# Loads of k, q and running sums for later query blocks issued from ScalarE's queue, in a hybrid decoder layer on one Trainium2 core

## The chip, the cores and the metric

The kernel runs on one core of one Trainium2 chip. A core has TensorE (PE in the profile; its weight loads have a row of their own, PEld), VectorE (DVE), ScalarE (ACT), GpSimd (POOL) and SyncE (SP), each with its own instruction queue that is worked off in order, and 16 DMA engines that move data between DRAM and the on-chip buffers. A DMA is started by an instruction in the queue of one of the engines. The metric is device time in microseconds of one launch. Before the change it is 2859.11 us, the median of 3 runs (2857.32 to 2863.01).

## The reference

One layer of a decoder trunk for 2048 positions of width 1024, in float32. A mixer with three head groups reads one projection; a SwiGLU block and a gated per-layer embedding follow. What matters here is the third head group, attention with a forget bias, six heads of 64, swept in query blocks, and what runs beside it:

```python
h = h + mixer(rmsnorm(h))                  # SSD group | RG-LRU group | attention, then w_out
u = rmsnorm(h, norm2_g)
h = h + (silu(u @ w_gate) * (u @ w_up)) @ w_down        # d_ff = 2816
u = rmsnorm(h, norm3_g)
h = h + sigmoid(u @ w_ple_gate + b) * (p @ w_ple_proj)
...
cum = cumsum(log_f)                                     # attention, per head
logits = q @ k.T / 8 + cum[q, None] - cum[None, k]      # k up to the end of the query block
probs = softmax(where(causal, logits, -inf))
out = probs @ v
```

## The kernel before

Positions lie on the free axis, in four blocks of 512 (`tb` 0 to 3, `TB` = 512); features lie on the 128 partitions. Every dense product is done as three matmuls (`mm3`, L199 to L201): weight and activation are each split in a high and a low half, and high·high, high·low and low·high are summed in PSUM. A weight tile goes through `wst` (DMA, L183, two buffers), ACT writes its high half (L189), POOL its low half (L190), and three such `w` tiles exist at a time. One weight is 24 matmuls of 512 columns.

Phase 1 makes k, q, v and the recurrent group, phase 1b the SSD group and the attention of query block 0. Phase 3 (`phase3`, L828) is the rest, and the change lies in it: for `tb` 0, 1, 2 the feed-forward of block `tb` is the main stream, and the attention of query block `tb+1` is a side stream (`attention_t`, L691). `attention_t` is a generator; `mm3` calls it forward by a few steps after each group of three matmuls. So the stretches of the trace with attention beside the feed-forward are three: 750 to 1160 us (query block 1), 1360 to 1680 us (block 2) and 1900 to 2290 us (block 3). They are called the first, second and third stretch below. The last feed-forward has no attention beside it.

For one head, `attention_t` does this. `load_keys` (L702) fills four tiles with one buffer each: `kx` (two DMAs of 64 partitions, the keys up to the end of the query block, L711), `qx` (two DMAs, L710), `qh` (two DMAs, L713) and `cum` (one DMA, the running sums copied to all partitions, L714), seven DMAs a head. `scores` takes the four 128-row tiles of the query block, the longest first: POOL adds the mask to a piece of `cum` (L733); PE makes four score pieces (L739 with `qx`, L740 with `qh`); DVE adds `cum` and takes the maximum (L741, L745); ACT does the exponential (L747) and, after a reciprocal on DVE (L749), the scaling (L750); DVE transposes in 32x32 pieces (L751); four DMAs store the tile to DRAM (`dp`, L753). `outputs` loads it back as `pT` (L769), ACT and DVE or POOL split it (`ph`, L776 and L777), and PE multiplies it with `vc`, the values (L720, one buffer, loaded once a head; L780 and L781). The result goes out as `dy` (L786). Since `kx`, `qx`, `qh` and `cum` have one buffer each, a head's load can start only when the last score of the head before has been computed, and the next head's first L739 needs all of `kx`.

The order within each engine's queue isn't written out in the kernel: a scheduler orders the instructions with estimates of its own for when each becomes ready, so that a change in who issues a DMA also moves compute instructions by some places. Before the change SP issues every transfer.

Of the kernel before, what the change touches and what calls it, by code (L numbers as in the profile page):

```python
# [11 lines left out]
F32 = mybir.dt.float32  # L12
# [7 lines left out]
P = 128  # L20
# [44 lines left out]
class Trunk:  # L65
# [625 lines left out]
    def attention_t(self, qc, pool, tags, tag_o):  # L691
# [3 lines left out]
        nc = self.nc  # L695
        K = (qc + 1) * NCH
# [5 lines left out]
        def load_keys(h):  # L702
            kx = self.t(pool, [P, K, 4, 32], "kx", F32R)
            cum = self.t(pool, [P, 4, K, 32], "cum")
            qx = self.t(pool, [P, TB], "qx", F32R)
            qh = self.t(pool, [P, TB], "qh", F32R)
            o = slice(64 * (h % 2), 64 * (h % 2) + 64)
            q, k = self.dq[h // 2, o, :, tsl], self.dk[h // 2, o, :, 0:K * P]
            for s in range(2):
                nc.sync.dma_start(qx[64 * s:64 * s + 64].bitcast(F32), q[:, s])  # L710
                nc.sync.dma_start(kx[64 - 64 * s:128 - 64 * s].bitcast(F32).rearrange("p a g i -> p (a g i)"), k[:, s])  # L711
            for s in range(2):
                nc.sync.dma_start(qh[64 - 64 * s:128 - 64 * s].bitcast(F32), q[:, s])  # L713
            nc.sync.dma_start(cum.rearrange("p g k i -> p g (k i)"), self.dcug[h, :, 0:K].rearrange("g k i -> g (k i)").partition_broadcast(P))  # L714
            keys[h] = kx, cum, qx, qh

        def load_values(h):
# [6 lines left out]
        def scores(h, hv):  # L724
            if hv:
                load_keys(h)
# [292 lines left out]
```

## Time and profile before

| | |
|---|---|
| median of 3 runs | 2859.11 us |
| the profiled execution | 2864.66 us, its span 2862.6 us |
| mean granted TensorE clock | 0.983 |
| ACT, DVE, POOL busy | 45%, 57%, 49% of the span |
| DMA issues on SP | 126 of them for `kx`, `qx`, `qh`, `cum` in `attention_t` |
| SP waits longest for | POOL L190 (1178.2 us at L183: it waits for a free weight buffer) |

The span runs from the first to the last instruction. Idle time of an engine that isn't waited for costs nothing; the granted clock is the share of its full speed at which TensorE was allowed to run.

### The profile page before, as it was taken

What the parts mean: (1) busy time and instruction counts of PE and PEld (TensorE: products, weight loads), DVE (VectorE), ACT (ScalarE), POOL (GpSimd) and SP (SyncE); (2) the same over time, 40 slices, a digit from 0 to 9 for tenths busy, and PEclk for the clock granted to TensorE, in tenths of its full rate; (3) what the DMA queues carried; (4) which work ended last, traced back from release to release, by engine and by line L of the source; (5) the groups of instructions that cost most, each with busy time, mean ns of one, the idle gap of its engine ahead of it and who ended that gap; (6) DMA issues with size and microseconds to landing.
All of it is one profiled execution on the core that took longest, in us unless ns stands there. A gap on an engine that the chain in (4) does not pass through costs nothing.

```text
span 2862.6 us, 36351 instructions
## 1 busy us (share of the span) xinstructions
PE 2745.4 (96%) x12845; PEld 2280.4 (80%) x12845; DVE 1636.1 (57%) x2740; ACT 1297.6 (45%) x1977; POOL 1407.3 (49%) x985
## 2 busy tenths in 40 slices
PE   7999999998989999999899999999999999999997
PEld 5787787887878888888787888877788878888886
DVE  6887546766554543647666547467674565513246
ACT  4555535653344442435555434356564443322234
POOL 5334576655445444444445534445455544544443
PEclk8999999998999999999999999999999999999999
DMA  5444544452367663435898634369997532322231
GB/s 189 172 169 156 178 155 141 146 171 91 132 206 200 196 192 113 138 126 157 244 251 240 196 117 149 105 183 292 280 270 203 162 134 101 125 96 97 102 96 67
DMA packets 319504, 467.93 MB, mean 163 GB/s; under 512 B 54196, under 2 KB 212948, under 8 KB 317780
## 3 DMA queue, kind: packets, MB, share of 16 engines
q1 hardware_dynamic: 319322, 465.60, 52.7%
q8 instruction: 102, 1.67, 0.2%
q14 instruction: 80, 0.66, 0.1%
HBM read 371.62 MB, written 93.88 MB: 163 GB/s over the span
## 4 chain that ended last, share of the span: by engine, by line
PE 65%; DMA 10%; DVE 9%; ACT 4%; POOL 4%; issue 4%; SPq 3%; DVEq 0%; POOLq 0%; ACTq 0%
PE mm L199 18%; PE mm L201 18%; PE mm L200 18%; DMA dp<-lg 2%; POOL w L190 2%; DMA kx<-dk 1%; DMA pT<-dp 1%; PE xd L781 1%; PE xd L780 1%; DMA cum<-dcug 1%; PE mm L217 1%; DMA ld<-dy 1%; PE mm L212 1%; SPq L753 1%; PE mm L213 1%
## 5 line engine op out<-in xcount | busy, mean ns | idle before, releaser
L190 POOL TENSOR_TENSOR w<-wst,w 128x1024 fp32r<-128x1024 f32 (+1 forms) x424 | 1018.8, 2404 | 994.0 <-ACT w L189 896.6
L199 PE MATMUL mm<-u,w 128*128 128x512 f32 (+1 forms) x3080 | 1207.6, 393 | 10.7 <-DVE h L487 4.5
L200 PE MATMUL mm<-u,w 128*128 128x512 f32 (+1 forms) x3080 | 1204.5, 391 | 0.9 <-DVE u L861 0.8
L201 PE MATMUL mm<-u,w 128*128 128x512 f32 (+1 forms) x3080 | 1204.5, 392 | 0.8 <-POOL w L190 0.7
L189 ACT ACTIVATE w<-wst 128x1024 fp32r<-128x1024 f32 (+1 forms) x424 | 440.3, 1039 | 541.1 <-PE mm L201 341.4
L199 PEld LDWEIGHTS mm<-u,w 128*128 128x128 f32 x3080 | 582.4, 189 | 122.8 <-ACT w L189 5.3
L201 PEld LDWEIGHTS mm<-u,w 128*128 128x128 f32 x3080 | 581.6, 189 | 117.9 <-POOL w L190 2.8
L200 PEld LDWEIGHTS mm<-u,w 128*128 128x128 f32 x3080 | 581.5, 189 | 110.2 <-DVE u L861 1.6
L861 DVE SCALAR_TENSOR_TENSOR u<-th,u 128x512 fp32r<-128x512 f32 x88 | 173.4, 1971 | 70.8 <-ACT u L860 70.7
L165 DVE TENSOR_TENSOR ssq<-ssq,sq 128x512 f32<-128x512 f32 x125 | 152.4, 1219 | 67.1 <-ACT sq L161 64.0
L777 DVE TENSOR_TENSOR ph<-pT,ph 128x512 fp32r<-128x512 f32 (+2 forms) x126 | 133.1, 1067 | 92.3 <-ACT ph L776 91.8
L777 POOL TENSOR_TENSOR ph<-pT,ph 128x512 fp32r<-128x512 f32 (+2 forms) x108 | 128.9, 1200 | 104.0 <-ACT ph L776 91.5
L776 ACT ACTIVATE ph<-pT 128x512 fp32r<-128x512 f32 (+2 forms) x234 | 118.2, 538 | 109.7 <-PE xd L781 51.3
L747 ACT ACTIVATE lg<-lg,m 128x1024 f32<-128x1024 f32 (+5 forms) x72 | 102.0, 1417 | 106.8 <-DVE m L745 94.8
L858 DVE TENSOR_TENSOR th<-th,mm 128x512 f32<-128x512 f32 x88 | 60.0, 682 | 153.9 <-PE mm L201 153.4
L751 DVE STREAM_TRANSPOSE lg<-lg 128x1024 f32<-128x1024 f32 (+5 forms) x72 | 113.4, 1575 | 46.9 <-ACT lg L750 46.9
L856 ACT ACTIVATE th<-mm 128x512 f32<-128x512 f32 x88 | 52.3, 594 | 169.2 <-PE mm L201 167.8
L874 DVE TENSOR_TENSOR h<-h,mm 128x512 f32<-128x512 f32 x96 | 65.2, 681 | 99.3 <-PE mm L201 99.1
L857 DVE SCALAR_TENSOR_TENSOR th<-th,mm 128x512 f32<-128x512 f32 x88 | 60.0, 682 | 106.2 <-ACT th L856 106.1
L780 PE MATMUL xd<-ph,vc 128*128 128x256 f32 (+1 forms) x396 | 105.6, 279 | 10.5 <-ACT ph L776 5.7
L781 PE MATMUL xd<-ph,vc 128*128 128x256 f32 (+1 forms) x396 | 103.4, 286 | 6.4 <-DVE ph L777 3.6
L750 ACT ACTIVATE lg<-lg,r 128x1024 f32<-128x1024 f32 (+5 forms) x72 | 101.7, 1412 | 13.2 <-DVE r L749 13.2
(319 smaller groups left out, 3336.8 us busy)
## 6 DMA issues: line engine op xcount, KB each, us to landing
wst<-in_w_gate SPq DMA_DIRECT2D x88, 512.0 KB, 3.5
wst<-in_w_up SPq DMA_DIRECT2D x88, 512.0 KB, 3.5
pT<-dp SPq DMA_DIRECT2D x162, 256.0 KB, 4.9
wst<-in_w_down SPq DMA_DIRECT2D x64, 448.0 KB, 3.4
wst<-in_w_out SPq DMA_DIRECT2D x32, 512.0 KB, 3.5
wst<-in_w_down SPq DMA_DIRECT2D x32, 512.0 KB, 5.5
wst<-in_w_pg SPq DMA_DIRECT2D x32, 512.0 KB, 3.4
vc<-dv SPq DMA_DIRECT2D x60, 256.0 KB, 5.2
```

Source lines behind the costliest of these rows:

```text
L165: (eng or nc.gpsimd).tensor_tensor(acc, acc, s, op=ALU.add)
L189: nc.scalar.activation(w[:, 0], st, ACT.Copy)
L190: nc.gpsimd.tensor_tensor(w[:, 1], st, w[:, 0].bitcast(F32), op=ALU.subtract)
L199: nc.tensor.matmul(ps, lhsT=w[:, 0, k], rhs=x[:, 0], start=k == 0, stop=False)
L200: nc.tensor.matmul(ps, lhsT=w[:, 0, k], rhs=x[:, 1], start=False, stop=False)
L201: nc.tensor.matmul(ps, lhsT=w[:, 1, k], rhs=x[:, 0], start=False, stop=k == len(u) - 1)
L751: nc.vector.transpose(lg, lg)
L776: nc.scalar.activation(hi, src, ACT.Copy)
L777: (nc.vector if t0 % 4 == 0 else nc.gpsimd).tensor_tensor(lo, src, hi.bitcast(F32), op=ALU.subtract)
L780: nc.tensor.matmul(po[:, sl], lhsT=vc[:, t0 + i], rhs=ph[:, 0, i, sl], start=t0 + i == 0, stop=False)
L781: nc.tensor.matmul(po[:, sl], lhsT=vc[:, t0 + i], rhs=ph[:, 1, i, sl], start=False, stop=t0 + i == KH - 1)
L861: nc.vector.scalar_tensor_tensor(hh[:, 1], th, 0.5, hh[:, 0].bitcast(F32), op0=ALU.mult, op1=ALU.subtract)
```

## The change

The seven DMAs of `load_keys` are issued from ACT's queue instead of SP's: six heads in three query blocks, 126 DMAs. Their sources, destinations and sizes are the same, and so is all that is computed. The loads for query block 0 (`attention`, L606) and every other transfer stay on SP.

```diff
             for s in range(2):
-                nc.sync.dma_start(qx[64 * s:64 * s + 64].bitcast(F32), q[:, s])
-                nc.sync.dma_start(kx[64 - 64 * s:128 - 64 * s].bitcast(F32).rearrange("p a g i -> p (a g i)"), k[:, s])
+                nc.scalar.dma_start(qx[64 * s:64 * s + 64].bitcast(F32), q[:, s])
+                nc.scalar.dma_start(kx[64 - 64 * s:128 - 64 * s].bitcast(F32).rearrange("p a g i -> p (a g i)"), k[:, s])
             for s in range(2):
-                nc.sync.dma_start(qh[64 - 64 * s:128 - 64 * s].bitcast(F32), q[:, s])
-            nc.sync.dma_start(cum.rearrange("p g k i -> p g (k i)"), self.dcug[h, :, 0:K].rearrange("g k i -> g (k i)").partition_broadcast(P))
+                nc.scalar.dma_start(qh[64 - 64 * s:128 - 64 * s].bitcast(F32), q[:, s])
+            nc.scalar.dma_start(cum.rearrange("p g k i -> p g (k i)"), self.dcug[h, :, 0:K].rearrange("g k i -> g (k i)").partition_broadcast(P))
```

The scheduler then orders the queues anew. At three places its new order is shown. In the rows, the numbers behind a name tell buffers apart.

The first place is TensorE at the start of the first stretch: `kx_7171` is the first head's, `mm_7287` and `mm_7349` are products of two feed-forward weights that follow each other.

```order
 L200 MATMUL mm_7287<-u_1459_6899,w_7284 128x512
 L201 MATMUL mm_7287<-u_1459_6899,w_7284 128x512
+L739 MATMUL xa_7186<-kx_7171,qx_7173 128x256
+L739 MATMUL xe_7196<-kx_7171,qx_7173 128x256
+L739 MATMUL xb_7206<-kx_7171,qx_7173 128x256
+L739 MATMUL xc_7216<-kx_7171,qx_7173 128x256
 L199 MATMUL mm_7349<-u_1445_6864,w_7346 128x512
```

The first four score matmuls stood behind 22 of the 24 matmuls of `mm_7349`, and now stand ahead of all of them.

The second place is the load of the third head of the second stretch (`kx_12431`). On SP before, `dp_12172` is the store of the probabilities of the second head and `pT_12378` a reload of the half before:

```order
L710 DMA qx_12433<-dq_81 64x512
L711 DMA kx_12431<-dk_82 64x1536
L710 DMA qx_12433<-dq_81 64x512
L711 DMA kx_12431<-dk_82 64x1536
L713 DMA qh_12434<-dq_81 64x512
L753 DMA dp_12172<-lg_12174 32x4x320 x4
L769 DMA pT_12378<-dp_11936 128x4x96
L769 DMA pT_12378<-dp_11936 128x4x128
L713 DMA qh_12434<-dq_81 64x512
L714 DMA cum_12432<-dcug_89 128x4x384
```

On ACT after the change, `lg_12174` and `lg_12223` are the last two score tiles of the second head:

```order
L750 ACTIVATE lg_12174<-lg_12174,r_12214 128x1280
L710 DMA qx_12433<-dq_81 64x512
L711 DMA kx_12431<-dk_82 64x1536
L710 DMA qx_12433<-dq_81 64x512
L711 DMA kx_12431<-dk_82 64x1536
L713 DMA qh_12434<-dq_81 64x512
L747 ACTIVATE lg_12223,l_12274<-lg_12223,m_12272 128x1152
L713 DMA qh_12434<-dq_81 64x512
L776 ACTIVATE ph_12141<-pT_12138 128x256
L776 ACTIVATE ph_12141<-pT_12138 128x128
L714 DMA cum_12432<-dcug_89 128x4x384
L750 ACTIVATE lg_12223<-lg_12223,r_12276 128x1152
```

The loads now stand between the scaling of the last but one tile and the exponential of the last one; nothing but them stands between the two halves of `kx`.

The third place is SP in the first stretch at the values of the second head (`vc_7888`); `lg_7763` is a score tile of that head.

```order
 L769 DMA pT_7946<-dp_7555 128x4x128
+L753 DMA dp_7761<-lg_7763 32x4x192 x4
 L720 DMA vc_7888<-dv_83 128x4x128 x2
-L183 DMA wst_8041<-in_w_gate 128x1024
 L786 DMA dy_84<-sq_7751 64x256
-L753 DMA dp_7761<-lg_7763 32x4x192 x4
```

The loads of `vc` are now behind the four stores of that tile, and the weight load `wst_8041` is ahead of them.

## The prediction

> **What bounds the kernel now.** I read the page's busy times first, then the windows by stretch, then TensorE's timeline for its gaps.
>
> ```profile
> span 2862.6 us, 36351 instructions
> PE 2745.4 (96%) x12845; PEld 2280.4 (80%) x12845; DVE 1636.1 (57%) x2740; ACT 1297.6 (45%) x1977; POOL 1407.3 (49%) x985
> ...
> 750.00:1160.00 410.00, 399.21 (x1904) 332.60 (x1903) 200.90 (x425) 176.02 (x267) 190.24 (x115) 0.99 0.59 177
> 1160.00:1360.00 200.00, 199.14 (x902) 165.40 (x902) 122.58 (x181) 87.63 (x119) 92.02 (x43) 1.00 0.45 141
> 1360.00:1680.00 320.00, 302.31 (x1456) 252.67 (x1455) 180.48 (x336) 157.76 (x225) 159.44 (x102) 0.98 0.77 221
> 1900.00:2220.00 320.00, 309.72 (x1470) 257.00 (x1469) 200.76 (x354) 184.14 (x230) 163.20 (x104) 0.99 0.89 258
> ```
>
> TensorE bounds it: busy 2745.4 of 2862.6 us. The windows (stretch and its length, busy time of PE, PEld, DVE, ACT, POOL, then granted clock, DMA share, GB/s) show what the change can reach: TensorE idles 410 - 399.21 = 10.8 us in the first stretch with attention, 17.7 in the second and 10.3 in the third, 38.8 in all. It executes the same matmuls afterwards, so the change can only fill or widen such gaps. The second row, without attention, gives the pitch of a matmul, 199.14 / 902 = 0.221 us. The gaps that hang on attention are these (start, duration, instruction, and in brackets the idle time ahead of it with what ended it):
>
> ```profile
> 820.22 0.38 PE L780 MATMUL xd<-ph,vc 128*128 128x256 f32 x1 [4.27 <-ACT ph L776]
> 829.05 0.36 PE L740 MATMUL xa<-kx,qh 128*128 128x256 f32 x1 [0.97 <-DMA qh<-dq]
> 857.40 0.36 PE L780 MATMUL xd<-ph,vc 128*128 128x256 f32 x1 [3.46 <-DMA vc<-dv]
> 1405.94 0.66 PE L739 MATMUL xa<-kx,qx 128*128 128x384 f32 x1 [5.41 <-DMA kx<-dk]
> 1449.62 0.66 PE L739 MATMUL xa<-kx,qx 128*128 128x384 f32 x1 [3.30 <-DMA pT<-dp]
> 1972.10 0.77 PE L739 MATMUL xa<-kx,qx 128*128 128x512 f32 x1 [2.71 <-DMA kx<-dk]
> 2060.53 0.47 PE L739 MATMUL xa<-kx,qx 128*128 128x512 f32 x1 [0.47 <-PE mm L201]
> ```
>
> Five are over 2.5 us, together 19.2 us, and three of these stand ahead of the first score of a new head, the instruction that needs the moved loads. (L739 reads no `pT`; its 3.30 us I put down to `kx`, whose second half was issued 6.15 us earlier, below.) A gap costs more than its length:
>
> ```profile
> 1404.00:1408.00 4.00, 2.06 (x6) 1.99 (x7) 0.97 (x3) 0.99 (x3) 3.57 (x2) 0.59 0.80 237
> 1408.00:1412.00 4.00, 4.00 (x11) 3.12 (x11) 0.20 (x1) 0.00 (x0) 0.00 (x0) 0.56 0.73 196
> 1447.00:1455.00 8.00, 5.38 (x20) 4.62 (x21) 3.72 (x3) 1.48 (x3) 2.96 (x3) 0.79 1.05 292
> 1970.00:1980.00 10.00, 7.91 (x26) 6.62 (x27) 3.91 (x6) 2.51 (x4) 3.94 (x3) 0.66 1.04 335
> ```
>
> Behind the gap at 1405.94 the granted clock is 0.59 and 0.56 for 8 us: (0.41 + 0.44) x 4 = 3.4 us lost; behind 1449.62 it is 0.79 over 8 us, 1.7 lost; behind 1972.10 it is 0.66 over 10 us, 3.4 lost. The Trainium skill (TensorE: Matmul & The Clock Gate, "Why this matters for your kernels") wants no gaps over about 3 us between bursts of matmuls. By that rule the 2.71 us gap would have cost no clock; here it did, and the row decides.
>
> **The change part by part.** What goes from SP and comes to ACT is 36 + 36 + 36 + 18 = 126 issues (minimum, median and maximum in ns):
>
> ```profile
> L710 SPq DMA_DIRECT2D qx<-dq x36: 450/513/1206, 783.4 to 2105.0; - x36
> L711 SPq DMA_DIRECT2D kx<-dk x36: 451/587/1432, 784.0 to 2105.6; - x36
> L713 SPq DMA_DIRECT2D qh<-dq x36: 445/594/918, 785.9 to 2111.0; - x36
> L714 SPq DMA_DIRECT2D cum<-dcug x18: 344/533/917, 787.2 to 2111.5; - x18
> ```
>
> At the medians that is 36 x (0.513 + 0.587 + 0.594) + 18 x 0.533 = 70.6 us of queue time, 3.9 us a head. No row shows an issue on ACT. It may hide behind a running ACTIVATE (nothing), or cost what SP's slowest cost: 36 x (1.206 + 1.432 + 0.918) + 18 x 0.917 = 144.5 us, 8.0 us a head. I take SP's medians, the same kind of instruction. ACT is busy 184.14 of 320 us in the third stretch; 3.9 us for each of some seven heads make that 211, two thirds. So beside its idle time the issues themselves cost nothing; if that cover were gone, the weight halves (L189) would come late by up to 3.9 us a head. No new wait goes ahead of other work of ACT by much: the loads wait for the last score of the old head, and the exponential of that score, which ACT waits for anyway, stands right behind them or among them. Behind ACT's loads queue L747 and L750 of that tile, whose stores and reloads TensorE needs, by the order, only about 40 us of matmuls later, and L856 and L189.
>
> *The third head of the second stretch*, the second place shown in the order (SP's rows, then ACT's):
>
> ```profile
> 1439.32 0.55 SPq L711 DMA_DIRECT2D kx<-dk  x1
> ...
> 1441.28 2.14 SPq L753 DMA_DIRECT2D dp<-lg  x4
> 1443.47 0.85 SPq L711 DMA_DIRECT2D kx<-dk  x1
> ...
> 1436.15 1.37 ACT L750 ACTIVATE lg<-lg,r 128x1280 f32<-128x1280 f32 x1 [0.23 <-DVE r L749]
> ```
>
> Between the halves of `kx` SP waited for and issued four stores. On ACT they follow L750, which ends at 1437.5; the loads still wait for the last score, as SP's first half did that left at 1439.32; one more issue of `qx` and one of `kx` behind it, at 0.55 each, bring the second half to about 1440.5, 3 us earlier than 1443.47. TensorE's first score of that head also comes 2.6 us of matmuls later in the new order, counted from the last score before (11.2 for 8.6). That covers 3.30: **-5.0 us** with its clock. If the DMA engines, at a share of 1.05 there, deliver no earlier, the order alone takes 2.6.
>
> *The values of the second head of the first stretch* (`vc`), the third place:
>
> ```profile
> 848.92 0.94 ACT L747 ACTIVATE lg<-lg,m 128x768 f32<-128x768 f32 x1 [1.23 <-DVE m L745]
> ...
> 854.53 0.92 ACT L750 ACTIVATE lg<-lg,r 128x768 f32<-128x768 f32 x1
> ...
> 852.21 0.99 SPq L720 DMA_DIRECT2D vc<-dv  x2
> ...
> 856.49 1.76 SPq L753 DMA_DIRECT2D dp<-lg  x4
> ```
>
> Now behind the stores, `vc` would go out later, had ACT's order not changed too: L750 of `lg_7763` stood behind two L776 until 854.53, and now follows L747 at about 850.2. The stores came 1.96 us after that start and take 1.76, so `vc` goes at 853.9, 1.7 later than 852.21; TensorE reaches its first use 4.8 us of matmuls later. 3.46 + 1.7 - 4.8 = 0.4 us are left of the gap. I take **-2.5** (bounds -5.2 with 1.7 of clock, +1.7 if the order's shift is lost).
>
> *The start of the first stretch*, the first place:
>
> ```profile
> 781.80 1.06 ACT L189 ACTIVATE w<-wst 128x1024 fp32r<-128x1024 f32 x1 [1.25 <-PE mm L217]
> 785.23 0.60 SPq L711 DMA_DIRECT2D kx<-dk  x1
> 791.99 0.28 PE L739 MATMUL xa<-kx,qx 128*128 128x256 f32 x1
> DMA to landing us min/median/max: 4.7/4.8/4.8
> ```
>
> The first scores move up by 22 x 0.221 = 4.9 us, to 787.1. ACT gets to the loads when its L189 ends at 782.9, so the second half of `kx` goes at about 784.7, hardly before 785.23, and lands 4.8 later at 789.5 to 790. A new gap of 2.5 to 3 us opens. The gap of 4.27 at 820.22 then shrinks, since TensorE arrives there later while the scores' chain doesn't: together **+1** (bounds: -2, and +4.7 with the clock).
>
> *The second heads* of the second and third stretch (1405.94 and 1972.10): of the latter, the old head's last score, SP's second half and ACT's L750:
>
> ```profile
> 1959.26 0.35 PE L740 MATMUL xc<-kx,qh 128*128 128x416 f32 x1
> 1963.13 0.59 SPq L711 DMA_DIRECT2D kx<-dk  x1
> 1963.71 1.80 ACT L750 ACTIVATE lg<-lg,r 128x1792 f32<-128x1792 f32 x1 [2.73 <-DVE r L749]
> ```
>
> The new order has the second half behind that L750, so 1 to 3 us later than SP; TensorE arrives 2.2 us later. At 1405.94 TensorE arrives 1.6 us earlier, and ACT's loads are spread around an L750 as well. **-1** for each; bounds 0 and the whole gaps with their clock, -8.8 and -6.1.
>
> *The fourth and fifth head of the third stretch* get their second half behind the exponential (L747) of the last score:
>
> ```profile
> 2046.74 0.35 PE L740 MATMUL xc<-kx,qh 128*128 128x416 f32 x1
> 2051.76 0.59 SPq L711 DMA_DIRECT2D kx<-dk  x1
> 2052.35 1.67 ACT L747 ACTIVATE lg<-lg,m 128x1664 f32<-128x1664 f32 x1
> ```
>
> There SP issued it at 2051.76, and ACT would at 2052.35 or, behind the whole L747, at 2054.0: 0.6 to 2.3 us later, for a gap that was 0.47: **+1.5**.
>
> Sum: -5.0 - 2.5 + 1 - 1 - 1 + 1.5 = **-7.0 us**. SP, freed of 70.6 us, brings nothing else that I can price; attention ends 10.7 us of matmuls later in the last stretch, with 33 us of matmuls still ahead of the first product that needs its result. The profiled execution took 2864.66 us, 2862.6 of span and 2.1 around it: 2857.7. That execution lies 5.55 us over the median of the runs shown, so the median becomes 2859.1 - 7.0 = **2852.1 us**.
>
> **The rivals.** *The DMA engines are the queue.* For it: the share is 0.89 over the third stretch and 1.04 to 1.05 where the gaps are. Then `kx` lands no sooner whoever issues it, and the small shifts cancel: 2859 us, within 2. Against it: between the halves at 1439.32 and 1443.47 SP waited, and no engine was asked to move that half. The Trainium skill has this as a rule (DMA: Bandwidth & Descriptors, "Issuing engines are not separate DMA queues"): transfers from several queues share the 16 engines, and only issue time is saved. The 0.89 agrees with it.
>
> *ACT becomes the slow queue.* The loads stand in order behind L750, L776 and L747, which themselves wait. Seven heads (one in the first, two in the second, four in the third stretch) have under 13.5 us of matmuls between the old head's last score and the new head's first, while SP's second half in the row above left 5.0 us after the score. With 7.5 us to land (6.15 from 1443.47 and 9.0 from 1963.13 to the ends of the gaps) it turns at 6 us: if ACT issues later than that, each stalls. Three us of stall and 1.7 of clock for seven are 33 us; the gaps that they replace (5.41, 3.30, 2.71, 0.97, 0.47, clock 8.5) take 21 off: +12, **2871**. Against it: ACT idles 42% there.
>
> *The full gain.* All five large gaps go, clock kept: -19.2, **2840**. Against it: the start and the second heads.
>
> **How the numbers follow.** Forecast 0.45, its own range 2846 to 2858; DMA engines 0.23; ACT slow 0.20; full gain 0.12. A measurement tells 0.2%, 5.7 us, from no change. Of the forecast two thirds lie under 2853.4 (0.30), with the full gain and a little of the second case 0.43 faster; slower is ACT's case with most of its chance, 0.18; 0.39 between. The range, 2840 to 2867, holds the forecast, the DMA case, half of the full gain and the lower half of ACT's case.
>
> **What would show it.** Right: no gap ahead of L739 near 1449, the gap near 857 under 1 us, a new one of about 3 us at 787 to 790, issues on ACT near 0.5 us, and under 38.8 us of TensorE's idle time in the three stretches. Wrong: issues on ACT over 1 us, or gaps ahead of L739 at most heads of the third stretch, or ACT's L189 late so that L199 waits.

## The result, and the profile after

The changed kernel takes **2876.94 us** (median of 6 runs, 2874.53 to 2879.49), the kernel before, run beside it, 2860.31 (6 runs, 2856.56 to 2863.01): a ratio of 1.0056, 95% interval 1.0044 to 1.0068. It is 16.6 us slower, where the prediction had 7 us faster. Its profiled execution took 2878.08 us.

The page's first lines after the change:

```profile
span 2876.3 us, 36333 instructions
PE 2743.9 (95%) x12845; PEld 2281.6 (79%) x12845; DVE 1626.8 (57%) x2740; ACT 1298.5 (45%) x1977; POOL 1402.1 (49%) x985
```

and the windows of the three stretches (columns as in the prediction):

```profile
750.00:1160.00 410.00, 393.72 (x1877) 327.17 (x1876) 188.10 (x422) 172.93 (x261) 186.07 (x114) 0.99 0.59 173
1360.00:1680.00 320.00, 306.60 (x1494) 258.21 (x1493) 185.79 (x346) 159.75 (x228) 162.92 (x103) 0.99 0.80 227
1900.00:2220.00 320.00, 304.80 (x1435) 254.51 (x1434) 198.18 (x347) 179.28 (x222) 157.38 (x101) 0.98 0.87 253
```

TensorE is as busy as before (2743.9 us against 2745.4); what grew is its idle time. It idles 16.3 us in the first stretch (10.8 before), 13.4 in the second (17.7) and 15.2 in the third (10.3): 44.9 for 38.8. Another 7 us came behind the third. Its gaps after the change:

```profile
796.90 0.55 PE L739 MATMUL xa<-kx,qx 128*128 128x256 f32 x1 [8.62 <-DMA qh<-dq]
869.82 0.36 PE L780 MATMUL xd<-ph,vc 128*128 128x256 f32 x1 [2.27 <-DMA vc<-dv]
1409.83 0.58 PE L780 MATMUL xd<-ph,vc 128*128 128x256 f32 x1 [5.07 <-ACT ph L776]
1924.01 0.58 PE L780 MATMUL xd<-ph,vc 128*128 128x256 f32 x1 [3.47 <-ACT ph L776]
1972.61 0.48 PE L739 MATMUL xa<-kx,qx 128*128 128x512 f32 x1 [2.64 <-DVE mx L741]
2004.90 0.72 PE L739 MATMUL xa<-kx,qx 128*128 128x416 f32 x1 [2.97 <-DVE mx L741]
2066.56 0.77 PE L739 MATMUL xa<-kx,qx 128*128 128x512 f32 x1 [3.53 <-issue]
2330.77 1.65 PE L199 MATMUL mm<-kx,w 128*128 128x512 f32 x3 [8.05 <-ACT kx L870]
```

The two largest are new, and stand at the two ends of what the change touches: ahead of the very first score, and 29 us behind the attention's last store. (L739 reads `kx` and `qx`, not `qh`; with the same loads alone on ScalarE, below, the same gap is put down to `kx`.) The last one is ahead of L199 reading the buffer `kx`: by then `phase3` has put `px` there, the per-layer input `pt`, split into two halves (L866 to L871), and L199 multiplies it by `w_pp` (the "em products" below). The granted clock behind these two gaps is the third number from the right:

```profile
797.00:801.00 4.00, 4.00 (x14) 3.34 (x15) 2.45 (x1) 0.53 (x2) 2.77 (x2) 0.62 0.60 156
2331.00:2340.00 9.00, 9.00 (x27) 7.39 (x28) 3.37 (x8) 1.28 (x3) 1.01 (x1) 0.53 0.44 146
```

0.53 over 9 us is another (1 - 0.53) x 9 = 4.2 us lost behind the 8.05.

Why the em products wait shows in SP's and ACT's rows ahead of them. `load_y` loads three tiles of the attention's result into the three `ld` buffers (L798), where they stay until they are normalized; `pt` is loaded into `ld` as well, so it waits for them. SP:

```profile
2301.70 0.45 SPq L786 DMA_DIRECT2D dy<-sq  x1
2303.96 0.33 SPq L799 DMA_DIRECT2D ld<-dy  x1
2326.79 0.99 SPq L799 DMA_DIRECT2D ld<-in_pt  x2
```

ACT:

```profile
2324.34 1.95 ACT L171 ACTIVATE u<-ld,par 128x512 fp32r<-128x512 f32 x3 [2.09 <-DVE ld L814]
2330.09 1.25 ACT L870 ACTIVATE kx<-ld 128x512 fp32r<-128x512 f32 x2 [1.34 <-DMA ld<-in_pt]
```

The attention's last store at 2301.70, its reload, the norm, L171 that frees the buffers, the load of `pt` at 2326.79, its split at 2330.09, the product at 2330.77: a chain of 29 us. Before, it ran 14 us earlier, here with TensorE's only wait of over 0.3 us at the em products, 18 matmuls behind the first of them and for something else (L886 on ACT copies the result of an earlier em product out of PSUM):

```profile
2312.38 0.99 SPq L799 DMA_DIRECT2D ld<-in_pt  x2
...
2324.84 0.50 PE L199 MATMUL mm<-kx,w 128*128 128x512 f32 x1 [1.44 <-ACT lg L886]
```

The first em product ran at 2318.92 without a wait. From the load of `pt` to the product that needs it takes 2330.77 - 2326.79 = 4.0 us, so `px` was ready at about 2316.4: by this estimate the attention could have ended some 2.5 us later at no cost, and beyond that each us of delay is a us of wait.

In TensorE's list of instructions the attention's last product of the third stretch was row 10016 and is now row 10063, 10.7 us of matmuls later, while the em products kept their place. So the question for the runs: does the loss come from ScalarE's queue, or from the order that the scheduler made when the loads' queue changed?

### The profile page after: what moved, and what is told of

The parts are those of the page before. It is cut to its first block, busy times and chain, and to the rows that moved or that the text cites. A ratio compares the mean times of both kernels' runs of the same rounds, so it can differ in the third digit from the quotient of the medians.

```text
span 2876.3 us, 36333 instructions
## 1 busy us (share of the span) xinstructions
PE 2743.9 (95%) x12845; PEld 2281.6 (79%) x12845; DVE 1626.8 (57%) x2740; ACT 1298.5 (45%) x1977; POOL 1402.1 (49%) x985
## 3 DMA queue, kind: packets, MB, share of 16 engines
q8 instruction: 102, 1.67, 0.2%
## 5 line engine op out<-in xcount | busy, mean ns | idle before, releaser
L199 PE MATMUL mm<-u,w 128*128 128x512 f32 (+1 forms) x3080 | 1205.5, 392 | 12.3 <-DVE h L487 4.7
L199 PEld LDWEIGHTS mm<-u,w 128*128 128x128 f32 x3080 | 580.6, 189 | 123.5 <-ACT w L189 5.2
L861 DVE SCALAR_TENSOR_TENSOR u<-th,u 128x512 fp32r<-128x512 f32 x88 | 161.3, 1833 | 64.4 <-ACT u L860 64.4
L777 DVE TENSOR_TENSOR ph<-pT,ph 128x512 fp32r<-128x512 f32 (+2 forms) x126 | 138.2, 1110 | 103.5 <-ACT ph L776 98.9
L777 POOL TENSOR_TENSOR ph<-pT,ph 128x512 fp32r<-128x512 f32 (+2 forms) x108 | 128.7, 1198 | 132.7 <-ACT ph L776 126.6
L776 ACT ACTIVATE ph<-pT 128x512 fp32r<-128x512 f32 (+2 forms) x234 | 118.6, 538 | 134.2 <-PE xd L781 59.4
L856 ACT ACTIVATE th<-mm 128x512 f32<-128x512 f32 x88 | 52.2, 594 | 184.1 <-PE mm L201 171.7
L857 DVE SCALAR_TENSOR_TENSOR th<-th,mm 128x512 f32<-128x512 f32 x88 | 59.9, 682 | 114.7 <-ACT th L856 114.7
L780 PE MATMUL xd<-ph,vc 128*128 128x256 f32 (+1 forms) x396 | 105.6, 279 | 12.3 <-ACT ph L776 8.9
L781 PE MATMUL xd<-ph,vc 128*128 128x256 f32 (+1 forms) x396 | 102.1, 283 | 6.2 <-DVE ph L777 3.7
L750 ACT ACTIVATE lg<-lg,r 128x1024 f32<-128x1024 f32 (+5 forms) x72 | 101.8, 1413 | 12.8 <-DVE r L749 11.8
```

Of the source, the lines that this page charges most:

```text
L199: nc.tensor.matmul(ps, lhsT=w[:, 0, k], rhs=x[:, 0], start=k == 0, stop=False)
L776: nc.scalar.activation(hi, src, ACT.Copy)
L777: (nc.vector if t0 % 4 == 0 else nc.gpsimd).tensor_tensor(lo, src, hi.bitcast(F32), op=ALU.subtract)
L780: nc.tensor.matmul(po[:, sl], lhsT=vc[:, t0 + i], rhs=ph[:, 0, i, sl], start=t0 + i == 0, stop=False)
L781: nc.tensor.matmul(po[:, sl], lhsT=vc[:, t0 + i], rhs=ph[:, 1, i, sl], start=False, stop=t0 + i == KH - 1)
L861: nc.vector.scalar_tensor_tensor(hh[:, 1], th, 0.5, hh[:, 0].bitcast(F32), op0=ALU.mult, op1=ALU.subtract)
```

## The experiments

All are timed against the kernel before, run beside them, in five rounds. To see where time goes, the third column cuts each profiled execution at the em products: from the last small product ahead of the first stretch to the em products behind it, then to those behind the second and the third, each with TensorE's idle time in it (all from the windows). A section is one execution; the ratio holds 6 to 12. The last column is TensorE's longest wait at the em products. It holds two different waits: those of 2.67 us and more stand ahead of the first em product and are for `px` (L870); those under 2 us stand 18 matmuls behind it and are for L886, and there is then no wait for `px`. Across chips and runs the kernel before spread from 2853 to 2877 us.

| kernel | ratio, 95% | three sections, us / idle | em wait |
|---|---|---|---|
| before | 1 | 421.4/11.6, 557.4/18.6, 568.2/10.4 | 1.44 |
| changed | 1.0056, 1.0044–1.0068 | 427.6/17.1, 547.0/14.1, 583.1/23.8 | 8.05 |
| first_only | 1.0040, 1.0026–1.0053 | 429.3/16.4, 553.8/17.1, 570.3/13.1 | 1.86 |
| mid_only | 0.9988, 0.9975–1.0002 | 421.1/10.8, 551.3/14.9, 570.3/12.5 | 1.58 |
| last_only | 1.0062, 1.0041–1.0082 | 423.1/12.8, 553.6/18.7, 589.0/27.3 | 7.36 |
| pt_own_buffer | 1.0023, 1.0013–1.0033 | 425.2/15.5, 551.7/14.7, 580.7/18.9 | under 1 |
| first_head_SP | 1.0039, 1.0026–1.0052 | 421.6/11.5, 545.4/11.2, 586.4/25.5 | 7.65 |
| last_on_SP | 1.0012, 1.0001–1.0024 | 427.7/16.4, 559.6/19.3, 569.0/13.1 | 1.41 |
| before_two_kq_buffers | 1.0007, 0.9997–1.0018 | 425.6/11.4, 546.7/12.0, 576.0/17.0 | 1.58 |
| after_two_kq_buffers | 1.0014, 1.0003–1.0026 | 429.1/16.9, 546.8/13.1, 576.5/16.4 | 1.60 |
| scalar_rate44 | 1.0032, 1.0020–1.0045 | 428.2/16.6, 549.2/13.3, 577.8/17.7 | 1.66 |
| SP_late_end | 1.0041, 1.0028–1.0053 | 421.4/10.8, 549.5/16.0, 582.0/22.5 | 2.67 |
| mid_rate47 | 1.0010, 0.9995–1.0025 | 420.1/10.1, 551.2/14.3, 576.7/17.0 | under 1 |
| first_SP_rate44 | 1.0028, 1.0018–1.0038 | 421.8/10.8, 544.9/10.0, 584.2/22.9 | 1.57 |
| scalar_old_order | 1.0036, 1.0023–1.0050 | 425.4/15.1, 552.5/18.7, 580.3/18.7 | 1.67 |
| SP_new_order | 1.0077, 1.0058–1.0095 | 422.6/10.1, 553.2/18.8, 590.8/29.4 | 7.73 |
| scalar_third_old | 1.0026, 1.0012–1.0040 | 422.0/13.4, 550.0/14.7, 574.8/16.2 | 1.48 |
| repaired | 1.0019, 1.0006–1.0032 | 426.2/15.6, 544.7/10.0, 577.7/19.2 | 1.54 |
| mix | 0.9986, 0.9972–1.0001 | 423.4/10.9, 547.3/12.4, 570.9/15.2 | 1.59 |

**Which stretch.** Three kernels move the loads of one stretch only:

```diff
-            o = slice(64 * (h % 2), 64 * (h % 2) + 64)
+            o, eng = slice(64 * (h % 2), 64 * (h % 2) + 64), nc.scalar if qc == 1 else nc.sync
```

with `eng.dma_start` in the seven loads, and 2 or 3 for the 1.

> Only the 42 loads of the first stretch (qc 1) go to ScalarE; the other 84 stay on SP. Theory (the loss sits in two places: the start of the first stretch, and the em products behind the third): the whole cost of the start and nothing else, +7 us against the kernel before, 2867; the wait of about 8 us ahead of the first L739 near 797 is there, and the one of 8.05 us ahead of the em products (L199 out of kx, near 2331) is not. Rival 1 (every issue on ScalarE costs a like amount, so the 17 us go by the number of loads): a third, +5.5 us. Rival 2 (the cost goes by bytes over two rings, and kx and cum grow with 8, 12 and 16 key tiles): +3.7 us. Time alone can hardly tell these three; the places of the waits do.

> Only the 42 loads of the second stretch (qc 2) go to ScalarE. Theory: this stretch gained 8.7 us in the changed kernel between two matmuls that both kernels share, and neither of the two places that lose is touched: 2851 to 2854, 6 to 9 us faster than before. Rival 1 (cost by the number of issues): +5.5 us slower. Rival 2 (cost by bytes): +5.6 us slower.

> Only the 42 loads of the third stretch (qc 3) go to ScalarE. Theory: PE's row for the last product of that attention stands 47 rows (10.7 us of matmuls) later as in the changed kernel, the three ld buffers come free later, px is late, and the em products wait about 8 us with a half clock behind it: +14 us, 2874. Rival 1 (by issues): +5.5 us, no gap ahead of the em products. Rival 2 (by bytes): +7.5 us, spread over the heads of the stretch, no gap ahead of the em products.

The losses stand where the theory put them: the wait of 8 us ahead of the first score only with the first stretch's loads on ScalarE, the one at the em products only with the third's. TensorE's row in first_only, and in last_only:

```profile
799.09 0.55 PE L739 MATMUL xa<-kx,qx 128*128 128x256 f32 x1 [8.43 <-DMA kx<-dk]
```

```profile
2340.43 1.65 PE L199 MATMUL mm<-kx,w 128*128 128x512 f32 x3 [7.36 <-ACT kx L870]
```

Both lose some 4 us more than expected (11 and 18 us), and the middle stretch gains 3 us, not 6 to 9; its interval takes in no change. A cost by issues or bytes is out as the whole account: the same number of loads loses in two stretches and not in the other. Nor do the stretches add: 4.0 - 1.2 + 6.2 is 9.0 in a thousand, for 5.6 with all three. Each kernel has an order of its own; in the second stretch of mid_only about 110 of 2512 matmuls stand elsewhere than in the changed kernel.

**The em wait taken out, by a buffer.**

```diff
-                        y = self.load(a["pt"][k, :, tsl])
+                        nc.sync.dma_start(y := self.t(two, [P, TB], "th"), a["pt"][k, :, tsl])
```

> The changed kernel, with one edit: the two tiles of the per-layer input that px is made of are loaded into the th buffers instead of the ld buffers, so that they need not wait until the attention's output has been normalized. Theory: the gap of 8.05 us ahead of the em products and the half clock behind it (6.8 us lost) go, 2862 to 2865; the wait of the mix products for the attention's output may show in their place with 0 to 4 us. Rivals 1 and 2: the gap is only where a delay of the loads shows; taken away, it comes back at the mix products, 2874 to 2878.

The wait is gone and doesn't come back at the later products; the ratio falls from 1.0056 to 1.0023, 9.4 us. That was less than the 12 to 15 expected: the section of the third stretch is still 580.7 us with 18.9 idle. A part of the loss is in the heads.

**The start, and the last stretch undone.** `nc.sync if qc == 1 and h == 0 else nc.scalar`, and `nc.scalar if qc < 3 else nc.sync`:

> The changed kernel, but the seven loads of the first head of the first stretch stay on SP; the other 119 go to ScalarE. Theory: the first scores stand where they stood before (22 matmuls later in PE's order than in the changed kernel), their loads have SP's ring ahead of the value and weight loads again, and the wait of 8.6 us ahead of the first L739 near 797 goes; the section from the end of the work before to the first em products falls from 427.6 to about 422 us: 5 to 7 us faster than the changed kernel, 2871. The third stretch still loses. Rival (the loads on a second ring are late at every head, the first is only one of them): 1 to 2 us faster than the changed kernel, 2875.

> The first and second stretch's 84 loads on ScalarE, the third stretch's 42 on SP. Theory (costs are local to a stretch and its order): third stretch as before the change, no wait of 7 to 8 us ahead of the em products, so before + 7 (start) - 5 (second stretch) = +2, 2862, and 15 us faster than the changed kernel. Rival (cost by the number of issues): two thirds of the loss stay, 2871.

With the first head on SP the wait at the start is gone (first section 421.6), and the first scores are back behind the 22 matmuls, so this run undoes queue and order together. Some 5 us go with it (1.0039 against 1.0056; the intervals overlap a little). With the last stretch on SP its section is that of before (569.0) and 13 us are back.

**Two buffers each** for `kx`, `qx` and `qh` (`bufs=2`), with the loads on SP and on ScalarE:

> The kernel before (all loads on SP) with two buffers each for kx, qx and qh, so that a head's k and q can be loaded while the scores of the head before still read theirs; cum keeps one. Theory (what the first scores of a head wait for is the time from the last read of the single buffer to the landing of the next load, about 10 us of it load, whichever engine issues it): the waits ahead of L739 of 5.41, 3.30, 2.71, 1.92 and 1.22 us and the half clock behind them go, about 15 us with the clock, less what cum's single buffer puts in their place: 2845 to 2855. Rival (the wait is for SP's queue): the waits stay, 2858 to 2862.

> The changed kernel (all loads on ScalarE) with two buffers each for kx, qx and qh. Theory (the queue matters only through when a load is issued, and with a second buffer that is no longer what the first scores wait for): as the kernel before with two buffers, but for the start of the first stretch, +5 to 7 us: 2850 to 2860, 17 us or more faster than the changed kernel; PE's order has the attention of the third stretch end where it did before the change, so no wait of 7 us ahead of the em products. Rival (loads on ScalarE's ring land late or cost ACT whatever the buffers): 12 us or more behind the kernel before with two buffers.

The waits for `kx` are gone, but neither is faster than the kernel before. The theory's number was wrong: other waits come in their place. In the kernel before with two buffers TensorE's two largest in the third stretch are now

```profile
1974.08 0.58 PE L781 MATMUL xd<-ph,vc 128*128 128x256 f32 x1 [4.39 <-POOL ph L777]
...
2027.28 0.74 PE L739 MATMUL xa<-kx,qx 128*128 128x480 f32 x1 [4.47 <-DVE mx L741]
```

But the pair says something else: in both, the attention ends at row 10016, and the second and third sections are the same with the loads on SP and on ScalarE (546.7 and 546.8, 576.0 and 576.5); only the first differs, with the wait at the start (425.6 and 429.1). TensorE's order in them is not the same in the two kernels.

**The place of the end, moved by one number** in `rate` (L846), which says how fast attention is interleaved:

```diff
-                rate = 6 * (2 * (8 + 1) + 8 * (tb + 1) + 6) / RATE
+                rate = 6 * (2 * (8 + 1) + 8 * (tb + 1) + 6) / (RATE if tb < 2 else 44)
```

> The changed kernel (all 126 loads on ScalarE); one number differs: the rate at which the third stretch's attention is interleaved (divisor 44 in place of 45 for the last of the three blocks). PE's order is that of the changed kernel up to the fourth head of that stretch, and then the attention's last product is row 10016, as before the change, in place of 10063. Theory (the wait ahead of the em products comes from how late PE's order ends the attention, not from the engine that issues loads): the wait of 8.05 us falls to 1 to 2, and the changed kernel's loss shrinks by about 15 us: 2862. Rival (the loads on ScalarE make it, whatever the order): the wait stays, 2874 to 2877. Between them, as the run with px's own buffer: the em wait goes, and 7 to 9 us stay in the heads of the stretch: 2868.

> The kernel before (all loads on SP) with the same divisor at 36: PE's order then ends the third stretch's attention 22 rows (5 us of matmuls) later, at row 10038 in place of 10016, still with every load on SP. Theory: the wait ahead of the em products, 1.4 us in the kernel before, grows to 4 to 6 us, with a half clock behind it: 5 to 10 us slower than before, 2867. Rival (it is the queue): no such wait, 2860.

> Loads on ScalarE in the second stretch alone, and the divisor at 47, with which PE's order ends the third stretch's attention 44 rows (10 us of matmuls) earlier than before the change, row 9972. Theory: the 1.4 to 1.6 us wait ahead of the em products goes too, with the slow clock behind it, and the second stretch keeps its gain: 0.2 to 0.4% under the kernel before, 2850 to 2855. Rival (the em wait is hidden at 1.5 us already, and an earlier end packs the heads closer, so that they wait more): 2858 to 2862.

> The changed kernel with both repairs: the first head of the first stretch on SP, and divisor 44 in the third. Theory (costs are local and add): 2862 - 5 = 2857, at or a little under the kernel before. Rival (a loss in every head with its loads on ScalarE): 2865 or more.

The wait for `px` follows the row at which the attention ends, with either queue: none at rows 9972 and 10016, 2.67 us at 10038, 7.4 to 8.05 at 10063. The 2.5 us of slack estimated above fit: 5 and 10.7 us of matmuls later leave 2.5 and 8.2. (The 1.4 us that two of these expectations start from is the other wait, for L886.) But it isn't all. scalar_rate44 came back by 7 us, not 15, and first_SP_rate44 by 8, not 20. SP_late_end moved no load and lost 0.41%; its wait for `px` is 2.67 us, TensorE's idle time in the section grew by 12. And mid_rate47, with no wait at the em products, isn't faster than mid_only (1.0010 against 0.9988, the intervals overlap). The interleaving of the third stretch before the change was a good one: no other order of TensorE tried there took less than 576.0 us, and with it and loads on SP the section took 568 to 571 in all five profiles.

**Queue and order crossed.** For this TensorE's instructions were pinned, row for row, to the order of the kernel before or of the changed one, by edges that order issue without waiting (other engines' orders were left to the scheduler; in these profiles all matmuls carry one line, L1036, of the helper that records them):

```diff
-        Trunk(tc, aps, out).build()
+        trunk = Trunk(tc, aps, out)
+        trunk.build()
+        by = {r.ins.name: r.ins for r in trunk.nc.seen}
...
+        for x, y in zip(names[:-1], names[1:]):
+            tc.add_manual_dep(by[y], x, mybir.DependencyInfo(mybir.DependencyClass.NoSync, mybir.DependencyReason.DATA), reason="order")
```

> All 126 loads on ScalarE as in the changed kernel, with TensorE's instructions pinned to the order of the kernel before, row for row, by issue-order edges. Theory (order): the third stretch is as before, 568 to 571 us between the second and the third em products with PE idle about 11 to 13, no wait of 8 us ahead of the em products; at the start of the first stretch the loads still land later than from SP, so a wait of 3 to 4 us in place of 8.6; the total 2858 to 2864. Rival (queue): the third stretch still takes 577 or more, total 2870 or more.

> All loads on SP as in the kernel before, with TensorE's instructions pinned to the order of the changed kernel, row for row. Theory (order): it loses as the changed kernel does though no load moved: the third stretch 580 to 589 us, the wait ahead of the em products 7 to 8 us, and a wait of 4 to 5 us at the start of the first stretch (scores 4.9 us of matmuls earlier, loads landing as before); total 2868 to 2876. Rival (queue): 2858 to 2862, no such waits.

> The changed kernel, with TensorE's instructions pinned to the order of the kernel before in the third stretch and the em products behind it alone (rows 7900 to 10300). Theory (order): third stretch 568 to 571 us in place of 583, no wait of 8 us at the em products, the start of the first stretch as in the changed kernel: 2861 to 2864. Rival (queue): 2870 to 2877.

> Both losses taken out: the first head of the first stretch on SP, all other loads on ScalarE, and TensorE's order in the third stretch pinned to that of the kernel before; the second stretch has the changed kernel's order. Theory: sections of 421.5, 547 to 551 and 569 us, against 421.4, 554 to 557 and 568 before: 3 to 7 us under the kernel before, 2854. Rival (a loss in every head with loads on ScalarE): 2862 or more.

The section of the third stretch in SP_new_order (no load moved), and its em products:

```profile
1746.67:2337.42 590.75, 561.37 (x2609) 467.14 (x2607) 348.48 (x539) 294.58 (x387) 284.09 (x162) 0.98 0.69 198
```

```profile
2337.42 1.65 PE L1036 MATMUL mm<-kx,w 128*128 128x512 f32 x3 [7.73 <-ACT kx L870]
```

and in scalar_old_order (all loads moved, old order):

```profile
1750.82:2331.14 580.32, 561.67 (x2609) 466.24 (x2608) 342.05 (x539) 293.33 (x385) 279.93 (x161) 0.98 0.69 200
```

So both theories hold a part. TensorE's new order with every load on SP loses 0.77%, no less than the change itself (the intervals overlap), and makes the wait for `px`: that wait is the order's. ScalarE's queue with TensorE's old order loses 0.36%: 10 us that the theory of the order had at about nothing. The two don't add.

But the cross holds TensorE alone. The pins leave the other engines to the scheduler, and there the orders differ: in the third section of scalar_old_order, scalar_third_old and repaired, about 34 of ACT's 390 instructions, 50 of DVE's 542, 18 of POOL's 162 and 26 of SP's 336 other DMAs stand elsewhere than before the change, while the unpinned kernels with that section's order of TensorE and loads on SP have every engine's order as it was. So the 0.36% is the queue's together with what the scheduler did to the other engines because of it, and no run parts the two. Nor was a kernel pinned to its own order timed.

The cross settles the start of the first stretch better. First score of SP_new_order, then ACT and TensorE in scalar_old_order:

```profile
789.33 0.49 PE L1036 MATMUL xa<-kx,qx 128*128 128x256 f32 x1 [3.27 <-issue]
```

```profile
784.02 0.49 ACTq L710 DMA_DIRECT2D qx<-dq  x1
...
790.90 0.41 ACTq L714 DMA_DIRECT2D cum<-dcug  x1
791.35 1.08 ACT L856 ACTIVATE th<-mm 128x512 f32<-128x512 f32 x2 [7.50 <-DMA vc<-dv]
```

```profile
792.73 6.91 PE L1036 MATMUL mm<-u,w 128*128 128x512 f32 x22 [4.58 <-DVE th L857]
```

With the scores early and the loads on SP the first score waits 3.27 us (4 to 5 expected) and runs 7.01 us after the first load; in the changed kernel, at the same place of TensorE's order, 8.62 and 12.75. So 3.3 us of that wait come with TensorE's order and 5.4 with the loads on ScalarE and what the scheduler did to the other engines. And with the scores late and the loads on ScalarE they don't wait, but TensorE does, 22 matmuls ahead of them: L856, the activation of the feed-forward, stands behind the seven loads in ACT's queue, which take from 784.02 to 791.31 there (783.40 to 787.74 on SP before). It ran at 783.03 before the change and runs at 791.35 here; L857 waits for it, and TensorE for L857, 4.58 us.

Pinning the third stretch alone brings the change from 1.0056 to 1.0026; with the first head on SP as well, 1.0019, not the gain that was expected.

**The candidate that is left**, with loads on ScalarE only where they didn't lose (`nc.sync if qc == 3 or (qc, h) == (1, 0) else nc.scalar`):

> Loads on ScalarE in the first stretch from its second head on and in the second stretch (77 of 126); the first head of the first stretch and the whole third stretch on SP. PE's order is the changed kernel's in the second stretch and the one of before in the third. If sections add: 421.5, 545 to 552 and 569 to 570 us against 421.4, 554 to 557 and 568 to 570 with all loads on SP: 2 to 10 us under the kernel before, 2855. If the second stretch's gain is only the spread between runs (545 to 560 us with one and the same order so far): 2859 to 2862.

1.4 in a thousand under the kernel before, its interval up to 1.0001: not shown to be faster; mid_only gave nearly the same. Its second stretch has the order of mid_only, not that of the changed kernel as expected, and the expectation's "545 to 560 us with one and the same order" holds several orders. Mix and repaired differ by 0.33%, 9 us; between them lie the queue of the third stretch, the order of ACT, DVE, POOL and SP in it, and those 110 matmuls of the second.

**What ScalarE's queue costs.** Eight kernels have the old order in the third stretch, five with its loads on SP and three on ScalarE. For the four heads whose loads go out between 1900 and 2065 us I took from their rows when the last score had read the old `kx`, when the first load was issued, and when the first score ran (means of 20 and of 12 heads):

| loads from | buffer free to issue | issue to first score | free to first score |
|---|---|---|---|
| SP (before, first_only, mid_only, last_on_SP, mix) | 1.8 us | 10.8 us | 12.7 us |
| ScalarE (scalar_old_order, scalar_third_old, repaired) | 0.3 us | 12.8 us | 13.1 us |

ScalarE issues 1.5 us sooner, as the change would have it, and the first score runs 2.0 us later after it. Half a us of these 2.0 is the time until the second half of `kx` is issued (2.6 us after the first load, 2.1 on SP). It is worst at the head whose scores begin near 1975. ACT in scalar_old_order:

```profile
1963.05 0.45 ACTq L710 DMA_DIRECT2D qx<-dq  x1
1964.69 0.18 ACT L747 ACTIVATION_READ_ACCUMULATOR lg<-lg,m 128x1 f32 x1
1965.10 1.80 ACT L750 ACTIVATE lg<-lg,r 128x1792 f32<-128x1792 f32 x1 [0.23 <-DVE r L749]
1965.16 0.45 ACTq L711 DMA_DIRECT2D kx<-dk  x1
...
1967.02 0.45 ACTq L711 DMA_DIRECT2D kx<-dk  x1
```

The second half of `kx` goes 4.0 us after the first load, because L750 and its wait for DVE stand between; SP took 1.8 there. The landing itself hardly differs. DMA issues in the third stretch, of before and of after (queue: packets, MB, share; issue: count, size, median to landing):

```profile
q1 hardware_dynamic: 74686, 82.27, 89.1%
...
kx<-dk SPq DMA_DIRECT2D x10, 512.0 KB, 7.0
```

```profile
q1 hardware_dynamic: 69024, 67.53, 72.4%
q10 hardware_dynamic: 3120, 13.11, 14.3%
...
kx<-dk ACTq DMA_DIRECT2D x10, 512.0 KB, 6.8
```

One queue at 89% became two at 72 and 14, and `kx` takes 6.8 us for 7.0. The Trainium skill (DMA: Bandwidth & Descriptors, "Issuing engines are not separate DMA queues") has it that DMAs started by several engines run on the same 16 DMA engines, and that this saves only the time of issuing. These rows agree with it.

A net 0.4 us a head is not the 8 us by which the mean section of these three kernels is longer (577.6 us for 569.7). TensorE's order is the same in all eight, so its waits can be set side by side, matmul by matmul. Its idle time in the section is 5.2 us longer, and the larger part of that is not ahead of the scores, which read the moved loads (mean 11.9 us for 10.1), but ahead of L780 and L781 (5.3 for 2.0; 4.8 to 6.0 in the three, 1.2 to 2.4 in the five). Those wait for the reloaded probabilities, split by L776 on ACT and L777 on DVE or POOL, and some of these splits are among the instructions that stand elsewhere in ACT's, DVE's and POOL's order. That speaks for the other engines' order as a cause beside the queue; it isn't shown by a run.

## Why the prediction was wrong

- *TensorE bounds it; gaps decide, with a slow clock behind them.* Right: TensorE's idle time grew by 6 us in the stretches and 7 behind them, and the profiled execution by 13.4.
- *An issue costs ACT what it costs SP, about half a us.* Right, from the issue rows of the changed kernel:

```profile
L710 ACTq DMA_DIRECT2D qx<-dq x36: 452/476/1197, 784.2 to 2104.7; - x36
L711 ACTq DMA_DIRECT2D kx<-dk x36: 452/554/1452, 784.7 to 2105.4; - x36
```

- *Third head of the second stretch, -5.0.* The gap went as predicted: none ahead of L739 near 1449, and the clock from 1450 to 1464 is 1.00. But waits of 1.94 and 1.91 us for the splits of L777 came ahead of L781 at 1452.20 and 1460.12, so little idle time was saved. The section took 544.7 to 550.0 us in six profiles with the changed kernel's order in it, 549.5 to 557.4 in three with everything in it as before.
- *`vc` of the second head of the first stretch, -2.5.* Wrong in size: 2.27 of the 3.46 us stay.
- *Start of the first stretch, +1.* The place and the kind of the new gap were right, its size was not: 8.62 us in place of 2.5 to 3. The prediction took 4.8 us for the landing, measured when SP sent these loads ahead of everything else, and with the loads on SP the moved-up scores do wait 3.27 us (SP_new_order). On ScalarE SP sends its own loads at the same time, and ACT's are spread out. SP, then ACT:

```profile
784.59 0.98 SPq L720 DMA_DIRECT2D vc<-dv  x2
785.68 0.61 SPq L183 DMA_DIRECT2D wst<-in_w_up  x1
```

```profile
784.15 0.49 ACTq L710 DMA_DIRECT2D qx<-dq  x1
...
786.34 0.45 ACTq L711 DMA_DIRECT2D kx<-dk  x1
788.06 1.24 ACTq L713 DMA_DIRECT2D qh<-dq  x2
```

  From the first load to the first score it was 12.75 us, against 7.01 in SP_new_order: the landing was mis-sized by over 5 us. That sharing with `vc` and `wst` makes it late is argued from these rows, not shown apart. The Trainium skill (DMA: Bandwidth & Descriptors, section "Queues, rings and completion order") has it that an engine with work from several queues takes packets from them in turn; 12.75 for 7.01 us fits that, and no run here isolates it.
- *Second heads, -1 each* (the prediction counts these heads from zero). Near in size, and by luck: 5.41 and 2.71 became 5.07 and 2.64, but the first now stands ahead of L780 and is for L776, the second is put down to DVE; neither is put down to `kx`.
- *Fourth and fifth head of the third stretch, +1.5.* Too small: the fourth head's gap is 3.53 us, for 0.47.
- **The step that failed:** "attention ends 10.7 us of matmuls later in the last stretch, with 33 us of matmuls still ahead of the first product that needs its result". The first product that reads the attention's result is that far; but the em products, right behind the last `w_down` product, need the three `ld` buffers which that result occupies. So the later end, past some 2.5 us of slack, costs them 8 us and the clock: pt_own_buffer shows that the buffers make the wait, and SP_new_order that it comes with TensorE's order while every load is on SP. The prediction had seen the shift, and followed the data but not the buffers.
- *Beside ACT's idle time the issues cost nothing.* Wrong as well, and the second step that failed. The prediction named L856 among what queues behind the loads and put it at nothing; in scalar_old_order it runs some 8 us later, behind them, and TensorE waits 4.58 us for what needs it. With TensorE's order held the loss is 0.36%, how much of it by the queue itself and how much by the other engines' new order stays open.
- Of the rivals, the slow queue of ACT gave the nearest time, 2871, by another mechanism than what was found: in the third stretch it issues 0.3 us after the buffer is free, not 6. That the DMA engines are the queue holds for the landing there, 6.8 us for 7.0, and not at the start of the first stretch.

## What to carry to other kernels

Where a scheduler orders the program, moving a DMA to another queue changes the order of every engine; compare both orders, and price a shift at each later product not only by the data that it reads but by the buffers that must be free for it. To tell a queue's cost from the order's, pin the order and cross the two, and pin every engine's, or what the scheduler does to the others is counted as the queue's. A load that leaves a queue also stops holding back what stood behind it there, and holds back what stands behind it in the new one; look at both.

## What was unexpected in the hardware

TensorE's clock fell to 0.53 for 9 us behind an 8.05 us gap, so that gap cost over 12 us. The length of a gap alone doesn't set the clock: behind the 2.71 us at 1972.10 before the change it was 0.57 over the next 7 us, behind the 2.64 us at 1972.61 after it 1.00. And one execution tells little below 10 us: with the same order of every engine and the same queue (mid_only, mid_rate47, last_on_SP, mix) the second section took 547.3 to 559.6 us.
